# Moving the byte phase of the matmul streams and of the weights' low halves in a two-block hybrid network

## The chip, the cores and the metric

The kernel runs on one core of one Trainium2 chip. The metric is the device time of one execution in microseconds (us), taken as the median of several runs. TensorE does the matrix products, VectorE (DVE), ScalarE (ACT) and GpSimd (POOL) do elementwise work, and SyncE's queue (SP) issues the DMA transfers from device memory (HBM) into the on-chip buffer (SBUF, 128 partitions). TensorE writes its results into PSUM.

## The reference

The input is one sequence of 256 tokens with 2048 features in float32. Two residual blocks follow, and each is a mixer and a gated feed-forward network of width 5632, with an RMS norm ahead of each and one at the end:

```python
for i in range(DEPTH):                       # DEPTH = 2
    if i % 2 == 0:
        h = h + conv_pool_mixer(h, ...)      # w_in 2048x3072, 31-tap conv, pooling, w_out 2048x2048
    else:
        h = h + short_conv_mixer(h, ...)     # w_in 2048x6144, 3-tap conv, w_out 2048x2048
    h = h + swiglu(rms_norm(h, ffn_norm[i]), w_gate[i], w_up[i], w_down[i])
return rms_norm(h, final_norm)
```

All weights together are 5904 blocks of 128x128 float32, 387 MB, and each block is used for exactly one product with the 256 tokens.

## The kernel before

**Two halves for each number.** TensorE gets its operands in the type float32r, into which float32 is rounded. To keep the precision, each weight block and each activation is split: the high half is the rounded value, the low half is the float32 remainder, rounded in its turn. A product is hi times x-hi, plus hi times x-lo, plus lo times x-hi.

**How a product is issued.** `product` (lines 171 to 178) has two forms. The narrow one issues three matmuls of 256 columns (lines 176 to 178), each with its own weight load, all into one accumulator. It serves mixer 0 and the last output chunk of the last projection. The wide one issues two matmuls: the high weights against 512 columns (x-hi and x-lo side by side, line 173), and the low weights against the 256 columns of x-hi (line 174), which go into the second half of the accumulator. It serves everything else. TensorE loads the weights of a matmul while the matmul before it still streams: the low block is loaded while line 173 streams 512 columns, and the next product's high block while line 174 streams 256.

**How the weights come.** SP's queue fetches units of 16 blocks (1 MB) into four tiles `w` (line 114). `prepare` (lines 116 to 132) makes pieces of 8 blocks: ScalarE rounds `w` into a tile `hi` (line 124), and VectorE, or GpSimd for some pieces of mixer 0, subtracts into a tile `lo` (line 131). There are six tiles of each, and pieces are prepared four ahead. The blocks lie one behind another in a tile, 512 bytes each per partition. The order of the work is written out in the program: `next_block` hands out one block after another, and `tick` lets elementwise steps of mixer 0 in between.

**How the activations lie.** A stream is a chunk of 512 columns, 2048 bytes per partition: 1024 bytes of high halves and 1024 of low halves. Chunks lie one behind another in a room that is a little larger than they need; `moving(room, at, n)` (line 222) starts them `at` bytes into the room. The rooms are `xs` (the normed input of each mixer and network), `cat` (mixer 0's output), `y` (the hidden layer of a feed-forward network, one half of its width at a time) and `z` (the short-convolution mixer's output).

**Where everything lies.** Tiles are packed per partition one behind another, pool after pool, in steps of 32 bytes. All blocks and chunks have sizes that are multiples of 512, so one number per tile, its start modulo 512, says how a stream lies against the weights. Before the change the starts are, in bytes of a partition:

| what | start of the tile | offset `at` | modulo 512 | past the high halves, modulo 512 |
|---|---|---|---|---|
| hi (6 tiles of 4096) | 101952 | | 64 | 0 |
| lo (6 tiles of 4096) | 126528 | | 64 | 0 |
| w (4 tiles of 8192) | 69184 | | 64 | 0 |
| xs in mixer 0 (narrow) | 36160 | 32 | 352 | 288 |
| xs in the wide part | 36160 | 160 | 480 | 416 |
| cat (narrow) | 184928 | 0 | 96 | 32 |
| y (wide) | 159392 | 64 | 224 | 160 |
| z (wide) | 159392 | 64 | 224 | 160 |

The pools are laid down in the order constants, `h`, `xs`, `w`, `hi`, `lo`, small temporaries, and then what belongs to one phase (`cat`, `y` or `z` among it).

Of the kernel before, what the change touches and what calls it, by code (L numbers as in the profile page):

```python
# [12 lines left out]
F32R = mybir.dt.float32r  # L13
# [4 lines left out]
P = 128  # L18
T = 256
D = 2048  # L20
NC = D // P
# [4 lines left out]
NH = NF // 2  # L26
# [38 lines left out]
UNIT_AT = [sum(UNITS[:u]) for u in range(len(UNITS))]  # L65

PIECE = 8
PIECES = [(u, o, min(PIECE, n - o)) for u, n in enumerate(UNITS) for o in range(0, n, PIECE)]

LOOK = 4  # L70
AHEAD = 1

# [3 lines left out]


XS_M0 = 32
XS_F0 = 160
XS_M1 = 160  # L80
XS_F1 = 160
Y_F0 = 64
Y_F1 = 64
Z_M1 = 64
CAT = 0

POOL_SPLIT = range(96, 24 * NC + 16 + 7 * NC + 8)
# [7 lines left out]
def block_kernel(ctx: ExitStack, tc: tile.TileContext, xT: bass.AP, xtok: bass.AP, vec: bass.AP, wall: bass.AP, out: bass.AP):  # L95
    nc = tc.nc
    const = ctx.enter_context(tc.tile_pool(name="const", bufs=1))
    act = ctx.enter_context(tc.tile_pool(name="act", bufs=1))
    wst = ctx.enter_context(tc.tile_pool(name="wst", bufs=4))
    whl = ctx.enter_context(tc.tile_pool(name="whl", bufs=6))  # L100
# [9 lines left out]
    def fetch(u):  # L110
        if u < len(UNITS) and u not in loaded:
            n, off = UNITS[u], UNIT_AT[u] * P * P
            loaded[u] = w = wst.tile([P, 16 * P], F32, name="w")
            nc.sync.dma_start(w[:, : n * P], wall[off : off + n * P * P].rearrange("(p f) -> p f", p=P))  # L114

    def prepare(i):
        if i >= len(PIECES) or i in ready:
            return
        u, o, n = PIECES[i]
        fetch(u)  # L120
        w = loaded[u][:, o * P : (o + n) * P]
        hi = whl.tile([P, PIECE * P], F32R, name="hi")
        lo = whl.tile([P, PIECE * P], F32R, name="lo")
        nc.scalar.copy(hi[:, : n * P], w)  # L124
        engine = nc.vector
        if UNIT_AT[u] + o in POOL_SPLIT:
            if relief:
                relief.pop()
            else:
                engine = nc.gpsimd  # L130
        engine.tensor_tensor(out=lo[:, : n * P], in0=w, in1=hi[:, : n * P], op=ALU.subtract)  # L131
        ready[i] = (hi, lo)

    def next_block():
        b, i = cursor
        at = UNIT_AT[PIECES[i][0]] + PIECES[i][1]
        if b == at + PIECES[i][2]:
            ready.pop(i)
            i, at = i + 1, b
        for j in range(i, i + LOOK + 1):  # L140
            prepare(j)
        if i + LOOK < len(PIECES):
            for u in range(PIECES[i + LOOK][0] + 1, PIECES[i + LOOK][0] + AHEAD + 1):
                fetch(u)
        cursor[:] = [b + 1, i]
        hi, lo = ready[i]
        o = (b - at) * P
        return hi[:, o : o + P], lo[:, o : o + P]
# [16 lines left out]
    def drain():  # L165
        while any(queues.values()):
            for q in queues.values():
                if q:
                    q.popleft()[1]()
# [10 lines left out]
    def matmul_chunks(xs, ks, n=1, wide=False, behind=None):  # L180


        accs = [ps.tile([P, 2 * T], F32, name="acc") for _ in range(n)]
        for i, k in enumerate(ks):
            first, last = i == 0, i == len(ks) - 1
            for acc in accs:
                hi, lo = next_block()
                product(acc, hi, lo, xs[:, k, :], first, last, wide)
                tick()
            if behind is not None:  # L190
                behind(k)
        return accs
# [10 lines left out]
    def split(dst, src, scale=None):  # L203

        if scale is None:
            nc.scalar.copy(dst[:, :T], src)
            nc.vector.tensor_tensor(out=dst[:, T:], in0=src, in1=dst[:, :T], op=ALU.subtract)
        else:
            nc.scalar.activation(dst[:, :T], src, AF.Copy, scale=scale)
            nc.vector.scalar_tensor_tensor(out=dst[:, T:], in0=src, scalar=scale, in1=dst[:, :T], op0=ALU.mult, op1=ALU.subtract)  # L210
# [6 lines left out]

    identity = v[:, VECS["identity"] :]
    h = act.tile([P, NC, T], F32, name="h")
    xs_room = act.tile([P, NC * 2 * T + 64], F32R, name="xs")  # L220

    def moving(room, at, n):

        return room[:, at // 4 : at // 4 + n * 2 * T].rearrange("p (c t) -> p c t", c=n)
# [99 lines left out]
    def project(src, ks, norm=None, wide=False, narrow_end=False):  # L324

        for n in range(NC):
            if narrow_end and n == NC - 1:
                wide = False
            (acc,) = matmul_chunks(src, ks, wide=wide)
            if wide:  # L330
                t = phase[0].tile([P, T], F32, name="cross", bufs=3)
                nc.scalar.copy(t, acc[:, T:])
                nc.vector.tensor_tensor(out=h[:, n, :], in0=h[:, n, :], in1=t, op=ALU.add)
            nc.vector.tensor_tensor(out=h[:, n, :], in0=acc[:, :T], in1=h[:, n, :], op=ALU.add)  # L334
            if norm is not None:
                norm.add(n)

    def scaled(acc, r, name, wide=False):
        if not wide:
            s = (phase[0] if name == "pv" else tmp).tile([P, T], F32, name=name, bufs=2)  # L340
            nc.vector.tensor_tensor(out=s, in0=acc[:, :T], in1=r, op=ALU.mult)
            return s
        s = summed(acc, name)
        nc.vector.tensor_tensor(out=s, in0=s, in1=r, op=ALU.mult)
        return s
# [3 lines left out]
    xs = norm.xs  # L349
# [20 lines left out]
    rowsq = const.tile([P, 2], F32, name="rowsq")  # L370
    load(0, 1)
    prepare(0)
    prepare(1)
    load(1, 1)
    prepare(2)
# [8 lines left out]
    with tc.tile_pool(name="m0", bufs=1) as m0, tc.tile_pool(name="ps_side", bufs=2, space=PSUM) as ps_side:  # L384
# [166 lines left out]
        drain()  # L551
        norm = Norm("ffn_norm0", XS_F0)
        project(cat, range(NA), norm)

    def swiglu(norm, following, at):
        with tc.tile_pool(name="ffn", bufs=1) as fp:
            phase[0] = fp
            y = moving(fp.tile([P, NH * 2 * T + 32], F32R, name="y"), at, NH)
            r = None
            for half in range(2):  # L560
                for f in range(NH):
                    (acc_g,) = matmul_chunks(norm.xs, every, wide=True)
                    (acc_u,) = matmul_chunks(norm.xs, every, wide=True)
                    if r is None:
                        r = norm.rstd()
                    gate = scaled(acc_g, r, "gate", True)
                    up = scaled(acc_u, r, "val", True)
                    nc.scalar.activation(gate, gate, AF.Silu)
                    nc.vector.tensor_tensor(out=up, in0=up, in1=gate, op=ALU.mult)
                    split(y[:, f, :], up)  # L570
                project(y, range(NH), following if half else None, wide=True, narrow_end=half and following.final)
# [3 lines left out]

    after = Norm("mix_norm_o", XS_M1)
    swiglu(norm, after, Y_F0)


    norm = Norm("ffn_norm1", XS_F1)  # L580
    with tc.tile_pool(name="m1", bufs=1) as m1:
        phase[0] = m1
        z = moving(m1.tile([P, NC * 2 * T + 32], F32R, name="z"), Z_M1, NC)
        pad = SW - 1
        r = None
        for c in range(NC):
            (acc_c,) = matmul_chunks(after.xs, every, wide=True)
            (acc_v,) = matmul_chunks(after.xs, every, wide=True)
            if r is None:
                r = after.rstd()  # L590
            cg = scaled(acc_c, r, "gate", True)
            vv = scaled(acc_v, r, "val", True)
            cv = m1.tile([P, pad + T], F32, name="cv", bufs=2)
            nc.gpsimd.memset(cv[:, :pad], 0.0)
            nc.vector.tensor_tensor(out=cv[:, pad:], in0=cg, in1=vv, op=ALU.mult)
            wc = VECS["conv_w_o"] + c * SW
            co = m1.tile([P, T], F32, name="co", bufs=2)
            nc.vector.tensor_scalar(out=co, in0=cv[:, :T], scalar1=v[:, wc : wc + 1], scalar2=None, op0=ALU.mult)
            for k in range(1, SW):
                nc.vector.scalar_tensor_tensor(out=co, in0=cv[:, k : k + T], scalar=v[:, wc + k : wc + k + 1], in1=co, op0=ALU.mult, op1=ALU.add)  # L600
            (acc_b,) = matmul_chunks(after.xs, every, wide=True)
            bg = scaled(acc_b, r, "pv", True)
            nc.vector.tensor_tensor(out=bg, in0=bg, in1=co, op=ALU.mult)
            split(z[:, c, :], bg)
        project(z, every, norm, wide=True)


    last = Norm("final_norm", final=True)
    swiglu(norm, last, Y_F1)
    halves = rsqrt_of(*last.sums, scale=1.0 / D, halves=True)  # L610
    with tc.tile_pool(name="fin", bufs=1) as fin:
# [91 lines left out]
```

## Time and profile before

| | |
|---|---|
| median of 3 runs | 2094.08 us (2093.9 to 2096.47) |
| the profiled execution | 2094.95 us, of which the span from first to last instruction is 2093.2 us |
| TensorE matmul busy | 2070.2 us, 99% of the span, mean granted clock 0.996 |
| weight loads busy (overlapping the matmuls) | 1850.5 us, 88% |
| VectorE, ScalarE, GpSimd busy | 66%, 51%, 10% |
| read from HBM | 391.39 MB, 188 GB/s over the span |

A group of instructions is given as line, engine, operation, output and inputs, shape and count, then the busy time in us and the mean duration of one in ns, then the engine's idle time just before and what ended it. PE is TensorE's matmul side and PEld its weight loads. Matmuls are pipelined: one takes longer from start to end than the distance between the starts of two, so the distance is what sets the time. A row of the timeline has the start in us, the duration in us, the engine, the line and the instruction.

### The profile page before, as it was taken

The page shows a single profiled execution, that of the slowest core. Times are in us where ns is not written, and L with a number is a line of the kernel's source. Part 1 is how long each engine was busy: PE and PEld are TensorE (multiplying, and loading weights), DVE is VectorE, ACT ScalarE, POOL GpSimd, SP SyncE. Part 2 cuts the span into 40 slices and gives each one's busy share as a digit, 9 for nine tenths or more (in the row PEclk, how much of TensorE's full clock was granted, in tenths as well). Part 3 has the DMA queues.
Part 4 walks back from the last instruction along what each step waited for, and adds up shares of the span by engine and source line. Part 5 has one row for each costly group of instructions (what it writes and reads, how often), then busy time and mean ns, then how long its engine had stood idle before and what let it go on. Part 6 is the DMA issues. An engine that isn't in the chain of part 4 may idle for free.

```text
span 2093.2 us, 31608 instructions
## 1 busy us (share of the span) xinstructions
PE 2070.2 (99%) x12584; PEld 1850.5 (88%) x12584; DVE 1383.1 (66%) x1979; ACT 1061.8 (51%) x1571; POOL 200.5 (10%) x180
## 2 busy tenths in 40 slices
PE   8998999999999999999999999999999999999998
PEld 8998988888888888888888888888888888888887
DVE  6998766666556666666777777766666556666654
ACT  7886654444444444455444445554444444444453
POOL 2995200000000000011000001100000000000011
PEclk9999999999999999999999999999999999999999
DMA  8555455555555455555555555455555555555551
GB/s 322 190 199 181 151 190 184 193 189 186 196 184 198 182 195 188 188 195 183 189 191 184 198 182 199 181 186 197 182 195 187 190 193 184 199 183 195 187 191 71
DMA packets 56884, 395.53 MB, mean 189 GB/s; under 512 B 6432, under 2 KB 7200, under 8 KB 9760
## 3 DMA queue, kind: packets, MB, share of 16 engines
q1 hardware_dynamic: 56736, 393.52, 51.9%
q8 instruction: 98, 1.61, 0.3%
q14 instruction: 50, 0.41, 0.1%
HBM read 391.39 MB, written 2.10 MB: 188 GB/s over the span
## 4 chain that ended last, share of the span: by engine, by line
PE 98%; DMA 1%; DVE 1%; ACT 0%; SPq 0%; issue 0%; DVEq 0%; ACTq 0%
PE acc L173 57%; PE acc L174 29%; PE acc L176 4%; PE acc L178 4%; PE acc L177 3%; DMA rows<-in_xtok 0%; DMA h<-in_xT 0%; DVE res L620 0%; ACT hi L124 0%; PE st L252 0%; DVE lo L131 0%; PE st L283 0%; SPq L114 0%; ACT conv L492 0%; PE idle L258 0%
## 5 line engine op out<-in xcount | busy, mean ns | idle before, releaser
L131 DVE TENSOR_TENSOR lo<-w,hi 128x1024 fp32r<-128x1024 f32 (+1 forms) x691 | 846.2, 1225 | 634.3 <-ACT hi L124 630.1
L124 ACT CAST hi<-w 128x1024 fp32r<-128x1024 f32 (+1 forms) x740 | 775.5, 1049 | 963.9 <-PE acc L173 615.9
L173 PE MATMUL acc<-xs,hi 128*128 128x512 f32 x3584 | 1243.2, 392 | 0.0
L174 PE MATMUL acc<-xs,lo 128*128 128x256 f32 x3584 | 1002.3, 280 | 0.0
L173 PEld LDWEIGHTS acc<-xs,hi 128*128 128x128 f32 x3584 | 672.7, 188 | 148.5
L174 PEld LDWEIGHTS acc<-xs,lo 128*128 128x128 f32 x3584 | 672.7, 188 | 0.1
L173 PE MATMUL acc<-y,hi 128*128 128x512 f32 x1386 | 480.4, 392 | 0.0
L174 PE MATMUL acc<-y,lo 128*128 128x256 f32 x1386 | 386.8, 280 | 0.0
L173 PEld LDWEIGHTS acc<-y,hi 128*128 128x128 f32 x1386 | 259.9, 188 | 57.2
L174 PEld LDWEIGHTS acc<-y,lo 128*128 128x128 f32 x1386 | 260.2, 188 | 0.4
L314 POOL TENSOR_TENSOR sumsq<-sumsq,sq 128x256 f32<-128x256 f32 x56 | 59.0, 1053 | 1593.0 <-ACT sq L312 1593.0
L176 PE MATMUL acc<-xs,hi 128*128 128x256 f32 x512 | 142.7, 282 | 5.2 <-ACT hi L124 4.2
L177 PE MATMUL acc<-xs,hi 128*128 128x256 f32 x512 | 142.2, 280 | 0.0
L178 PE MATMUL acc<-xs,lo 128*128 128x256 f32 x512 | 140.2, 282 | 0.1
L131 POOL TENSOR_TENSOR lo<-w,hi 128x1024 fp32r<-128x1024 f32 x49 | 118.5, 2440 | 41.4 <-ACT hi L124 41.3
L176 PEld LDWEIGHTS acc<-xs,hi 128*128 128x128 f32 x512 | 96.9, 190 | 6.1 <-ACT hi L124 4.8
L177 PEld LDWEIGHTS acc<-xs,hi 128*128 128x128 f32 x512 | 96.9, 189 | 0.0
L178 PEld LDWEIGHTS acc<-xs,lo 128*128 128x128 f32 x512 | 95.4, 190 | 0.5 <-DVE lo L131 0.5
L173 PE MATMUL acc<-z,hi 128*128 128x512 f32 x256 | 88.7, 392 | 0.0
L198 ACT COPY cross<-acc 128x256 f32<-128x256 f32 x224 | 81.4, 363 | 0.0
L174 PE MATMUL acc<-z,lo 128*128 128x256 f32 x256 | 71.4, 280 | 0.0
L334 DVE TENSOR_TENSOR h<-acc,h 128x256 f32<-128x256 f32 x112 | 47.2, 423 | 18.3 <-PE acc L178 11.9
(134 smaller groups left out, 1199.3 us busy)
## 6 DMA issues: line engine op xcount, KB each, us to landing
w<-in_wall SPq DMA_DIRECT2D x365, 1024.0 KB, 4.8
w<-in_wall SPq DMA_DIRECT2D x7, 512.0 KB, 7.3
rows<-in_xtok SPq DMA_DIRECT2D x2, 1024.0 KB, 8.1
h<-in_xT SPq DMA_DIRECT2D x7, 256.0 KB, 7.2
out<-res SPq DMA_DIRECT2D x2, 512.0 KB, 2.8
out<-res SPq DMA_DIRECT2D x2, 384.0 KB, 2.8
v<-in_vec SPq DMA_DIRECT2D x1, 260.0 KB, 6.6
h<-in_xT SPq DMA_DIRECT2D x2, 128.0 KB, 2.3
```

The costliest lines, as they stand in the source:

```text
L124: nc.scalar.copy(hi[:, : n * P], w)
L131: engine.tensor_tensor(out=lo[:, : n * P], in0=w, in1=hi[:, : n * P], op=ALU.subtract)
L173: nc.tensor.matmul(acc, hi, x, start=first, stop=False, skip_group_check=True)
L174: nc.tensor.matmul(acc[:, T:], lo, x[:, :T], start=False, stop=last, skip_group_check=True)
L176: nc.tensor.matmul(acc[:, :T], hi, x[:, :T], start=first, stop=False)
L177: nc.tensor.matmul(acc[:, :T], hi, x[:, T:], start=False, stop=False)
L178: nc.tensor.matmul(acc[:, :T], lo, x[:, :T], start=False, stop=last)
L198: nc.scalar.copy(t, acc[:, T:])
L314: nc.gpsimd.tensor_tensor(out=self.sums[0], in0=self.sums[0], in1=sq, op=ALU.add)
L334: nc.vector.tensor_tensor(out=h[:, n, :], in0=acc[:, :T], in1=h[:, n, :], op=ALU.add)
```

## The change

Nothing is added to or taken from the list of instructions; addresses change.

- The room `xs` grows from 64 to 128 spare elements, 256 bytes, so all that is laid down after it moves up by 256.
- Each `lo` tile grows by 128 elements, 512 bytes. In the wide part (blocks from 656 on) its data begins 192 bytes into the tile; in mixer 0 it begins at its start as before.
- The rooms `y` and `z` grow from 32 to 128 spare elements.
- The offsets of `xs` in the wide part go from 160 to 416, those of `y` and `z` from 64 to 320. `XS_M0` stays 32 and `CAT` stays 0.
- `y` may have its own offset for each half; both are 320. `_ffn` is not used.

```diff
+_m0, _ffn = 24 * NC + 16 + NC * NC, 3 * NH * NC
+LO_AT = {0: 0, _m0: 192}
 XS_M0 = 32
-XS_F0 = 160
-XS_M1 = 160
-XS_F1 = 160
-Y_F0 = 64
-Y_F1 = 64
-Z_M1 = 64
+XS_F0 = 416
+XS_M1 = 416
+XS_F1 = 416
+Y_F0 = (320, 320)
+Y_F1 = (320, 320)
+Z_M1 = 320
...
-        lo = whl.tile([P, PIECE * P], F32R, name="lo")
+        lo = whl.tile([P, PIECE * P + 128], F32R, name="lo")
+        at = LO_AT[max(b for b in LO_AT if b <= UNIT_AT[u] + o)] // 4
+        lo = lo[:, at : at + PIECE * P]
...
-    xs_room = act.tile([P, NC * 2 * T + 64], F32R, name="xs")
+    xs_room = act.tile([P, NC * 2 * T + 128], F32R, name="xs")
...
-            y = moving(fp.tile([P, NH * 2 * T + 32], F32R, name="y"), at, NH)
+            y_room = fp.tile([P, NH * 2 * T + 128], F32R, name="y")
             r = None
             for half in range(2):
+                y = moving(y_room, at[half], NH)
...
-        z = moving(m1.tile([P, NC * 2 * T + 32], F32R, name="z"), Z_M1, NC)
+        z = moving(m1.tile([P, NC * 2 * T + 128], F32R, name="z"), Z_M1, NC)
```

## The prediction

> **What bounds the kernel now.** I read the page's first and fourth parts first, then the groups by line and shape, then the timeline of TensorE in stretches without a gap.
>
> ```profile
> span 2093.2 us, 31608 instructions
> PE 2070.2 (99%) x12584; PEld 1850.5 (88%) x12584; DVE 1383.1 (66%) x1979; ACT 1061.8 (51%) x1571; POOL 200.5 (10%) x180
> PE 98%; DMA 1%; DVE 1%; ACT 0%; SPq 0%; issue 0%; DVEq 0%; ACTq 0%
> ```
>
> The chain that ends last is TensorE for 98% of the span. What does not change the pace of the matmuls, or stop them, does not change the time. The groups say which matmuls these are:
>
> ```profile
> L173 PE MATMUL acc<-xs,hi 128*128 128x512 f32 x3584 | 1243.2, 392 | 0.0
> L174 PE MATMUL acc<-xs,lo 128*128 128x256 f32 x3584 | 1002.3, 280 | 0.0
> L173 PE MATMUL acc<-y,hi 128*128 128x512 f32 x1386 | 480.4, 392 | 0.0
> L173 PE MATMUL acc<-z,hi 128*128 128x512 f32 x256 | 88.7, 392 | 0.0
> L131 DVE TENSOR_TENSOR lo<-w,hi 128x1024 fp32r<-128x1024 f32 x688 | 844.6, 1228 | 632.3 <-ACT hi L124 628.1 <-PE acc L174 3.6
> L174 PEld LDWEIGHTS acc<-xs,lo 128*128 128x128 f32 x3584 | 672.7, 188 | 0.1
> ```
>
> There are 3584 + 1386 + 256 = 5226 wide products, and no wide matmul waited for anything (idle 0.0). Their pace is read from starts. First a stretch of the timeline on `xs`, with its first two and last two rows; between them lie 59 pairs:
>
> ```profile
> 299.80 0.39 PE L173 MATMUL acc<-xs,hi 128*128 128x512 f32 x1
> 300.03 0.28 PE L174 MATMUL acc<-xs,lo 128*128 128x256 f32 x1
> ...
> 320.26 0.39 PE L173 MATMUL acc<-xs,hi 128*128 128x512 f32 x1
> 320.49 0.28 PE L174 MATMUL acc<-xs,lo 128*128 128x256 f32 x1
> ```
>
> 59 pairs in 20.46 us are 346.8 ns a pair. Over these 59 the mean distance from a line 173 to its line 174 is 229.2 ns (so much for 512 columns), and the rest, 117.6 ns, is the slot of the 256 columns. Then the same on `y`, first and last row, 44 pairs apart:
>
> ```profile
> 519.61 0.39 PE L173 MATMUL acc<-y,hi 128*128 128x512 f32 x1
> ...
> 534.86 0.39 PE L173 MATMUL acc<-y,hi 128*128 128x512 f32 x1
> ```
>
> That is 15.25 us / 44 = 346.6 ns. 5226 pairs at 346.7 ns make 1812 us of the 2093.2. One nanosecond a pair is 5.2 us, 0.25% of the time.
>
> **Is there time in a pair that is not the streaming itself?** A row of matmuls of another kind answers, the sums over features and the fillers at the end, which are plain float32:
>
> ```profile
> L283 PE MATMUL st<-diag,ones x10: 378/379/454, 40.3 to 1365.8; 128*128 128x256 f32 x10
> L258 PE MATMUL idle<-ones x16: 275/275/356, 2081.6 to 2083.4; 128*128 128x128 f32 x16
> 275.84 0.43 PE st L283 x2
> ```
>
> In the program there are five matmuls of line 283, and ten records: a float32 product runs as two records, and the third line (the chain of waits) gives 0.43 us for two, 0.215 each, nearly twice the 112 ns by which 392 exceeds 280. So such a record occupies the array about as a 512-column matmul would, and it lasts 379 where line 173 lasts 392; by the same reading line 258 lasts 275 where line 174 lasts 280. The wide matmuls thus carry some 13 and 5 ns that a stream of the same length need not have. What they are the trace does not say. A weight load runs beside each of them from its start, as the timeline has it for one pair:
>
> ```profile
> 742.17 0.39 PE L173 MATMUL acc<-xs,hi 128*128 128x512 f32 x1
> 742.17 0.19 PEld L174 LDWEIGHTS acc<-xs,lo 128*128 128x128 f32 x1
> 742.40 0.28 PE L174 MATMUL acc<-xs,lo 128*128 128x256 f32 x1
> 742.40 0.19 PEld L173 LDWEIGHTS acc<-xs,hi 128*128 128x128 f32 x1
> ```
>
> The stream and the load read two places of one memory at the same time, and their getting in each other's way is the candidate.
>
> **The change part by part.**
>
> *Phase of the streams on `xs`.* The room `xs` keeps its start; `hi` moves up by 256 (the room's growth), the offset by 416 - 160 = 256. Past the high halves it stays at 416. Cost nothing: nothing moves against anything.
>
> *Phase of `y` and `z`.* Their base moves up by 256 (the room `xs`) and 6 x 512 (the `lo` tiles), which is 256 modulo 512, as `hi` does; the offset goes from 64 to 320. So they go from 160 to 416. The trace has both phases: 346.8 ns at 416 (`xs`) and 346.6 at 160 (`y`). 1642 pairs times 0.2 ns is 0.3 us: nothing.
>
> *Phase of `xs` in mixer 0.* The offset stays, `hi` moves: 288 becomes 32, which is where `cat` is now. Both are in the trace, first the narrow products on `xs`, 93 starts apart, then those on `cat`, 96 apart:
>
> ```profile
> 127.84 0.28 PE L176 MATMUL acc<-xs,hi 128*128 128x256 f32 x1
> ...
> 138.68 0.28 PE L176 MATMUL acc<-xs,hi 128*128 128x256 f32 x1
> ```
>
> ```profile
> 241.80 0.28 PE L176 MATMUL acc<-cat,hi 128*128 128x256 f32 x1
> ...
> 253.00 0.28 PE L176 MATMUL acc<-cat,hi 128*128 128x256 f32 x1
> ```
>
> 10.84 / 93 = 116.6 ns and 11.20 / 96 = 116.7 ns. Cost nothing.
>
> *The low halves, 192 bytes on.* This is the one new thing. Until now `lo` and `hi` had the same phase everywhere, so no row shows a stream against two different ones. What changes is which bytes the load of a low block reads while line 173 streams: the stream lies 416 - 192 = 224 past the low halves instead of 416 (or 160). Under line 174 the next high block is loaded, at 416 as before. So the slot of 117.6 ns stays, and the slot of 229.2 is in play. Its bounds: on the good side line 173 falls to what line 283 shows, 392 - 379 = 13 ns x 5226 = 67.9 us saved. On the bad side the load costs the stream as much again, 13 ns more, 67.9 us lost. For a value between I take the stream's own marginal pace: 392 - 280 = 112 ns per 256 columns, so 512 columns take 224, and 229.2 - 224 = 5.2 ns is what the slot holds beyond it. I take these 5.2 ns as saved, because the slot of line 173 is the only one in which a stall can sit in front of a second half that no load disturbs: the load of 128 columns starts with the matmul, and the last columns of 512 stream alone. 5.2 x 5226 = 27.2 us.
>
> The Trainium skill speaks against this. "SBUF — State Buffer" (section "Who interferes with whom") gives TensorE two independent read ports, one for the moving operand and one for weight loads, and says that PE never waits on anyone; by it the phase is worth nothing and the sum is 0. Its page "TensorE: Matmul & The Clock Gate" (section "Wait — 56ns, not 53.3ns?") gives a warm matmul N / 2.4 GHz + about 2.5 ns, an estimate of 325 ns for a pair; the trace has 346.7 at a granted clock of 1.00, so here something costs 22 ns a pair that neither rule names.
>
> *Elementwise work.* VectorE writes `lo` at another phase; `w` and `hi`, which it reads, keep theirs to each other. ScalarE's work is the same. Price zero, and the cover is this window of the first feed-forward network and the mixer behind it (columns: PE, PEld, DVE, ACT, POOL busy, clock, DMA share, GB/s):
>
> ```profile
> 330.00:1150.00 820.00, 820.00 (x4735) 721.92 (x4734) 530.29 (x722) 388.10 (x551) 15.08 (x25) 1.00 0.52 189
> ```
>
> VectorE is idle for 290 of 820 us; a piece of 8 blocks takes TensorE 8 x 346.7 = 2774 ns, so there are 296 pieces and 0.98 us of slack for each. The subtraction of 1228 ns would have to become some 2.2 us before TensorE waited. A faster TensorE takes slack away: at 341.5 ns a pair 42 ns per piece. The DMA share would go from 0.52 to 0.53. No buffer is taken away and no wait added: every tile keeps its number of buffers.
>
> *Sum.* The profiled execution took 2094.95 us (2093.2 of it span); less 27.2 that is 2067.8. The median of the runs, 2094.08, lies 0.9 below it, so I predict 2067 us.
>
> **The rivals.**
>
> *Nothing moves (2094 us).* Each pair of phases in the trace gives one pace: 416 and 160 wide, 288 and 32 narrow. If no phase at all matters and the 13 ns belong to the float32r stream itself, the shift of `lo` is one more number without effect. For it: those four, and that the pace is the same in all wide stages. Against it: the two members of each pair differ by exactly 256, so a pattern that repeats every 256 bytes would hide in them, and 192 is no multiple of that. The Trainium skill's rule of separate ports is this rival. It takes in the case that the change does not do what it says (that the phases come out as before), which I think excluded by the starts.
>
> *Slower: the low load meets the stream.* Place: line 173, the load of the low block beside it. At the new distance of 224 the load and the stream go to the same part of the memory more often than at 416, and each meeting holds up the stream. It decides as soon as the new distance stalls the stream longer than the old one. Price by the rows: another 5.2 ns a pair gives 2094 + 27 = 2121 us, 13 ns gives 2162. If the stall were small, 1 ns, 2099. For it: the distance has never been in this trace. Against it: the old distance has no sign of being a best one either, with 13 ns over line 283.
>
> *The whole of it goes (2026 us).* Line 173 falls to 379 ns: 2094 - 68. For it: a stall that has one cause goes as a whole. Against it: line 174 keeps its 5 ns at the unchanged distance, so some of the excess belongs to any load beside a stream.
>
> **How the numbers follow.** Part of the stall goes (the forecast, 2067, and by itself from 2035 to 2089): 0.48. All of it goes: 0.08. Nothing moves: 0.27. Slower: 0.17. What this kernel's measurement tells from no change is about 0.2%, 4 us, so faster has 0.48 + 0.08 = 0.56, the same 0.27, slower 0.17. The range goes down to the bound 2026 and up past no change to 2106, which holds the slower case with up to 2.3 ns a pair; what lies beyond is 0.13 above and about 0.03 below.
>
> **What would show it.** In the changed trace the distance from line 173 to line 174 is the test: 224 ns instead of 229.2, with line 174 to the next line 173 still at 117 to 118, and the same for `xs`, `y` and `z`. The duration of line 173 should fall under 392. The narrow stage up to 256 us should end when it did, within 1 us. Line 131 on VectorE may move by some ns and nobody waits for it. I am wrong if the slot of line 174 is what changes (then the load of the high block was the one in the way), if `xs` and `y` come apart, or if TensorE shows new idle time ahead of line 173 or 174.

## The result and the profile after

The changed kernel takes 2103.49 us (median of 5 runs, 2103.14 to 2106.32) against 2096.47 us for the kernel before (median of its 5 runs, 2093.90 to 2096.86). The ratio is 1.0042, with a 95% interval of 1.0031 to 1.0053. It is slower by some 7 to 9 us: the medians differ by 7.0 and the spans of the two profiled executions by 8.2 (2101.4 us against 2093.2), and the ratio stands for 8.8. One execution of the fourteen kernels is left out of all ratios: of the four of the kernel described below that has streams and low halves at 64, one took 10228 us and the others 2059 to 2062, and no trace shows why.

The new code lines move the products: the line 173 of before is line 178, line 174 is 179, and line 131 is 136. First the head of the page of the changed kernel and its groups of the wide matmuls and of the subtraction:

```profile
span 2101.4 us, 31608 instructions
PE 2079.6 (99%) x12584; PEld 1852.1 (88%) x12584; DVE 1383.8 (66%) x1979; ACT 1061.3 (51%) x1571; POOL 200.5 (10%) x180
...
L178 PE MATMUL acc<-xs,hi 128*128 128x512 f32 x3584 | 1249.3, 393 | 0.0
L179 PE MATMUL acc<-xs,lo 128*128 128x256 f32 x3584 | 1002.7, 280 | 0.0
L178 PE MATMUL acc<-y,hi 128*128 128x512 f32 x1386 | 481.7, 393 | 0.0
L178 PE MATMUL acc<-z,hi 128*128 128x512 f32 x256 | 90.1, 396 | 0.0
L136 DVE TENSOR_TENSOR lo<-w,hi 128x1024 fp32r<-128x1024 f32 x688 | 844.9, 1229 | 638.7 <-ACT hi L129 634.4 <-PE acc L179 3.7
```

The work is the same, the counts are the same, and still no wide matmul waits (idle 0.0). What was lost lies in the pace, the distance from the start of one pair to the start of the next: line 178 lasts 393 to 396 ns where it lasted 392. But a mean hides what happened. These are TensorE's matmuls in five stretches of 100 us, first before (columns: stretch in us, its length, busy time and number of matmuls, granted clock, DMA share, GB/s):

```profile
300.00:400.00 100.00, 100.00 (x579) 1.00 0.52 190
600.00:700.00 100.00, 100.00 (x579) 1.00 0.53 190
1100.00:1200.00 100.00, 100.00 (x579) 1.00 0.53 190
1400.00:1500.00 100.00, 100.00 (x579) 1.00 0.53 190
1700.00:1800.00 100.00, 100.00 (x579) 1.00 0.52 190
```

and the same stretches after:

```profile
300.00:400.00 100.00, 100.00 (x570) 1.00 0.53 189
600.00:700.00 100.00, 100.00 (x585) 1.00 0.53 190
1100.00:1200.00 100.00, 100.00 (x570) 1.00 0.52 184
1400.00:1500.00 100.00, 100.00 (x570) 1.00 0.52 184
1700.00:1800.00 100.00, 100.00 (x584) 1.00 0.54 194
```

Before, every stretch holds 579 (2 x 100 / 0.3467 = 577, and those that reach over the edges). After, some hold fewer (570) and some more (584 or 585), at the same granted clock of 1.00, on the same tile `xs` and at the same phases. The timeline of the changed kernel gives both paces; a pace that holds for a whole stretch is called a cadence from here on. First row and last row of line 178 in a stretch of the slow kind, 50 pairs apart, and in one of the fast kind, 51 pairs apart:

```profile
299.87 0.40 PE L178 MATMUL acc<-xs,hi 128*128 128x512 f32 x1
...
317.47 0.40 PE L178 MATMUL acc<-xs,hi 128*128 128x512 f32 x1
...
699.66 0.39 PE L178 MATMUL acc<-xs,hi 128*128 128x512 f32 x1
...
717.17 0.39 PE L178 MATMUL acc<-xs,hi 128*128 128x512 f32 x1
```

17.60 / 50 = 352.0 ns and 17.51 / 51 = 343.3 ns a pair; before it was 346.7 everywhere. The mean distance from line 178 to line 179 is 234.2 ns at the slow cadence and 226.7 at the fast cadence (229.2 before), so most of the difference lies in the slot of the 512 columns.

Taken over the whole trace, the slow cadence holds from the spread of the first norm (275.6 us) to 513.8, from 876.3 to 1610.8 and from 1973.3 to the end of the wide part. Inside the second of these stretches the 19 pairs between the sums and the spread of a norm are fast, twice (from 1003.7 and from 1365.3 us). Everywhere else the fast cadence holds. Of 5206 pairs whose neighbours are regular, 3010 have the slow cadence and 2196 the fast one. 3010 x (352.0 - 346.7) = 16.0 us lost and 2196 x (346.7 - 343.35) = 7.3 us won (343.35 is the mean of the 2196) leave 8.7 us. The narrow part ended 0.45 us earlier (the first wide matmul starts at 256.05 instead of 256.50). That makes 8.25 us; the span grew by 8.2.

Where does the cadence change? Around 513.8 us the regular order high, low, high, low is broken. This is the changed kernel's timeline there:

```profile
513.18 0.40 PE L178 MATMUL acc<-y,hi 128*128 128x512 f32 x1
513.42 0.28 PE L179 MATMUL acc<-y,lo 128*128 128x256 f32 x1
513.54 0.63 PE L178 MATMUL acc<-y,hi 128*128 128x512 f32 x2
514.01 0.40 PE L179 MATMUL acc<-y,lo 128*128 128x256 f32 x2
514.25 0.40 PE L178 MATMUL acc<-y,hi 128*128 128x512 f32 x1
```

Two long matmuls follow each other and then two short ones. Probably the last product of the first output chunk, which needs the last chunk of `y`, is put between the halves of a product of the second; the trace does not name the chunks. Both kernels have five such places, one behind the start of each projection on `y` and `z`. At the head of three stages the order is broken twice more, by the sums of the norm (line 257) and, 20 pairs on, by their spread (line 288), which brings the norm's factors to all partitions. All changes of cadence lie at these eleven places. Not every place changes it: the sums of the first norm and the place on `z` did not.

### The profile page after: what moved, and what is told of

Read it like the earlier page. It is cut to its first block, busy times and chain, and to the rows that moved or that the text cites. A ratio compares the mean times of both kernels' runs of the same rounds, so it can differ in the third digit from the quotient of the medians.

```text
span 2101.4 us, 31608 instructions
## 1 busy us (share of the span) xinstructions
PE 2079.6 (99%) x12584; PEld 1852.1 (88%) x12584; DVE 1383.8 (66%) x1979; ACT 1061.3 (51%) x1571; POOL 200.5 (10%) x180
## 4 chain that ended last, share of the span: by engine, by line
PE 98%; DMA 1%; DVE 1%; ACT 0%; SPq 0%; issue 0%; DVEq 0%; ACTq 0%
PE acc L178 57%; PE acc L179 29%; PE acc L181 4%; PE acc L183 4%; PE acc L182 3%; DMA rows<-in_xtok 0%; DMA h<-in_xT 0%; DVE res L626 0%; ACT hi L129 0%; PE st L257 0%; DVE lo L136 0%; PE st L288 0%; SPq L117 0%; ACT conv L497 0%; PE idle L263 0%
```

## Experiments

Theory A: the shift of the low halves splits the pace into two cadences, and which one holds is a state that only an irregular place can change. Its rivals: B, the moved streams have a part in it; C, the two distances (stream past high halves, stream past low halves) set one pace each; D, the stage or the other engines' work in it decides; E, VectorE's writes at the new phase are in the way.

### The change in two halves

The first kernel undoes the shift of the low halves alone:

```diff
-LO_AT = {0: 0, _m0: 192}
+LO_AT = {0: 0, _m0: 0}
```

> The changed kernel with the low halves put back to the high ones' phase (offset 0 in the wide part too); the layout and the phases of the streams stay as changed (416 everywhere in the wide part, 32 in mixer 0). Theory A, the shift of the low halves alone splits the pace of the wide pairs into two cadences (343.3 and 352.0 ns in the changed trace): this kernel has one cadence again, 346.7 ns in xs, y and z, and takes the time of before within 0.2% (2090 to 2099 us). Rival B, the move of y and z from 160 to 416 or of mixer 0 from 288 to 32 has a part in it: two cadences or a pace other than 346.7 ns remain on y or z, or the narrow stage ends elsewhere, and the time stays 4 us or more above before.

Measured: 2094.62 us against 2094.34 before, ratio 1.0001 (0.9991 to 1.0011), one cadence at 346.7 ns in all wide stages.

The second puts that shift alone into the kernel before; streams stay at 416 on `xs` and 160 on `y` and `z`:

```diff
-        lo = whl.tile([P, PIECE * P], F32R, name="lo")
+        lo = whl.tile([P, PIECE * P + 128], F32R, name="lo")
+        at = LO_AT[max(b for b in LO_AT if b <= UNIT_AT[u] + o)] // 4
+        lo = lo[:, at : at + PIECE * P]
```

> The kernel before with nothing but the low halves of the wide part 192 bytes on: xs at 416 past the high halves (224 past the low ones), y and z at 160 past the high halves (480 past the low ones). Theory A: the stages on xs run at 343.3 or 352.0 ns a pair as in the changed kernel. If only the phase modulo 256 counts, y and z do so too and the time is that of the changed kernel, 2100 to 2106 us; if 512 counts, y and z have a pace of their own, and the stages on xs still show the two cadences. Rival B: without the moved y and z the pace on xs is 346.7 ns and the time that of before.

Measured: 2104.16 us, ratio 1.0047 (1.0032 to 1.0062). The trace has the same two cadences in the same stages, on `y` at 160 as on `y` at 416; only the first 31 pairs differ, which ran at 352 here and at 343.6 in the changed kernel. The whole loss belongs to the low halves, and B falls. For these cells only the phase modulo 256 counts.

### All distances in one run

Two kernels sweep the phases inside one execution. The streams' phases differ by stage, and `lo` begins at a place that depends on the block:

```diff
-LO_AT = {0: 0, _m0: 192}
+def low_at(b):
+    ...
+    start, n = max(s for s in STEPS if s[0] <= b)
+    i = (b - start) // n
+    return 32 * i if i < 16 else 192
...
-        at = LO_AT[max(b for b in LO_AT if b <= UNIT_AT[u] + o)] // 4
+        at = low_at(UNIT_AT[u] + o) // 4
```

> The changed kernel with the phases swept inside one run: in each wide stage the low halves go from 0 to 480 bytes past the high ones in steps of 32 (16 to 48 products each), and the stages' streams lie at 416, 0, 64, 128, 192, 256, 320 and 384 past the high halves (first network: xs 416, y 0 and 64; mixer 1: xs 128, z 192; second network: xs 256, y 320 and 384). Theory C, the two distances (stream to high, stream to low) set the pace: line by line the pair takes different times, between 341 and 360 ns, and the same pair of distances gives the same pace wherever it stands. Theory A, there are two cadences at one and the same pair of distances and the way in decides: some neighbours in the sweep keep a cadence over a change of the distance. If the two reads don't meet at all: 346.7 ns everywhere.

> The same sweep with the streams at the odd multiples of 32: first network xs 160, y 32 and 96; mixer 1 xs 224, z 288; second network xs 352, y 416 and 480. Theory C: the map goes on smoothly between the columns of the other sweep; the column 160 is like 416 where the low halves are not shifted (346.7 ns, as y before), and differs where 512 counts. Theory A: at 416 on y and a shift of 192 either 343.3 or 352.0 ns, not a value between. If the two reads don't meet at all: 346.7 ns everywhere.

Measured: 2108.46 and 2111.58 us (one run each). The table has the ns of a pair, the mean over the second half of each stretch, worked out from the starts in the two traces. Stretches that hold an irregular place are left out. Rows are the stream past the high halves, columns the low halves past the high ones, both modulo 256. Values that lie more than 1.2 ns apart in one cell are set side by side.

| | 0 | 32 | 64 | 96 | 128 | 160 | 192 | 224 |
|---|---|---|---|---|---|---|---|---|
| 0 | 347 / 354 | 347 | 347 | 347 | 347 | 347 | 351 | 353 |
| 32 | 347 | 347 | 349 | 347 | 347 | 350 | 347 / 353 | 353 |
| 64 | 349 / 354 | 349 | 340 / 350 | 347 | 347 | 349 | 347 | 350 |
| 96 | 350 | 353 | 347 | 349 | 347 | 349 | 353 | 347 |
| 128 | 351 | 351 | 347 | 347 | 352 | 351 | 347 | 352 |
| 160 | 347 | 351 | 353 | 348 | 353 | 347 | 352 | 347 / 348 |
| 192 | 353 | 353 | 350 | 347 / 353 | 353 | 350 | 340 | 347 |
| 224 | 347 / 353 | 348 / 351 | 347 / 350 / 353 | 347 / 353 | 350 | 351 | 347 / 350 | 352 |

The kernel before stands in row 160, column 0; the changed one in row 160, column 192. Of 312 stretches 122 lie within 0.5 ns of 346.7, 183 above 348 and 4 below 346, all four at 340.0. So phases do matter, a shift taken blindly is more likely to lose than to win, and the same cell can have two paces. C holds for most cells and fails for some: (64, 64) ran at 340.0 and at 350.0. There the low halves lay at 64 and at 320, but the next sweep has 350.0 at 64 too, so a phase modulo 512 is not the reason. In both sweeps the changed kernel's cell showed only its slow cadence, in every visit.

A third sweep goes in steps of 8 bytes around the two cells at 340.0; its edit is the same with other numbers (shown against the first sweep):

```diff
-    return 32 * i if i < 16 else 192
+    return ((128, 120, 128, 136, 144, 112, 0, 8, 0, 504)[STEPS.index((start, n))] + 8 * min(i, 15)) % 512
```

> A sweep like the two before, in steps of 8 bytes around the cells that ran at 340.0: streams at 192, 184, 200, 208 and 176 past the high halves in the first network and mixer 1, 64, 72 and 56 in the second network; the low halves go from 64 below the stream to 56 above it (the stream 64 to -56 past the low halves). Theory C: around 0 there is a stretch of some 16 to 48 bytes at 340 ns and no pair below it, and outside it up to 353. If 340 is not a floor, some cell goes below, down to 325 ns.

Measured: 2113.92 us (one run). There is no stretch of fast cells. With the stream at 192, the low halves 40 below the stream, 16 below it and 40 above it give 340.0, and the cells between give 347 to 353. Among these is (192, 192) itself, which had 340.0 in the first sweep and has 353 here, both times it comes up. Streams at 184, 200, 72 and 56, which are no multiples of 16, never reach 340; they lie between 346.6 and 366.6. But those at 208, 176 and 64, which are multiples of 16, do not reach it here either (346.5 to 355.5). Nothing goes below 340.0. The width that C expected is refuted, its floor held.

### Two cells applied everywhere

Both kernels change numbers only; this is the first, whose low halves stay 192 bytes on. The second has 64 in place of each 192, for the low halves too, and 480 in place of 96, which places `y` and `z` at 64.

```diff
-XS_F0 = 416
-XS_M1 = 416
-XS_F1 = 416
+XS_F0 = 192
+XS_M1 = 192
+XS_F1 = 192
...
-Y_F0 = (320, 320)
-Y_F1 = (320, 320)
-Z_M1 = 320
+Y_F0 = (96, 96)
+Y_F1 = (96, 96)
+Z_M1 = 96
```

> The changed kernel with other phases: all wide streams at 192 past the high halves (instead of 416), low halves 192 on as there, so that the stream lies at 0 past the low halves. In the sweep this cell ran at 340.0 ns a pair in mixer 1's z, both times it came up. Theory C (the two distances set the pace, with one cadence here): 340.0 ns in every wide stage, 5226 x 6.67 = 34.9 us under before, 2058 to 2062 us. Theory A (two cadences here too): 340 ns in some stages and 345 to 353 in others, 2065 to 2110 us.

Measured: 2111.81 us, ratio 1.0087 (1.0073 to 1.0101). Ahead of the first norm's sums 28 pairs ran at 340.0, and from these sums on all ran at 350.0. The cell that had 340.0 twice in the first sweep makes the slowest of the kernels with one set of phases.

> The changed kernel with all wide streams at 64 past the high halves and the low halves 64 on; again the stream lies at 0 past the low halves. In the sweep the cell (64, 64) and its like (320, 64) ran at 340.0 ns, the cells (64, 320) and (320, 320), which are the same modulo 256, at 350.0. Theory A: two cadences, 340.0 and 350.0, which change at the irregular places only, and a time between 2060 and 2112 us. Theory C: if 512 counts for the low halves, 340.0 throughout, 2058 to 2062 us.

Measured: 2061.57 us against 2094.67, ratio 0.9839 (0.9824 to 0.9854). This beats both kernels. Its groups and its timeline, 51 pairs between first and last row:

```profile
L178 PE MATMUL acc<-xs,hi 128*128 128x512 f32 x3584 | 1220.3, 389 | 0.0
L179 PE MATMUL acc<-xs,lo 128*128 128x256 f32 x3584 | 990.2, 276 | 0.0
```

```profile
699.83 0.39 PE L178 MATMUL acc<-xs,hi 128*128 128x512 f32 x1
...
717.17 0.39 PE L178 MATMUL acc<-xs,hi 128*128 128x512 f32 x1
```

17.34 / 51 = 340.0 ns, in every wide stage, but not for all of it. The first 31 wide pairs ran at 350.0, and so did the 19 pairs between the sums and the spread of each of the three norms. These are the first and the last of the 19 behind the second norm's sums, 18 pairs apart:

```profile
988.74 0.40 PE L178 MATMUL acc<-xs,hi 128*128 128x512 f32 x1
...
995.04 0.40 PE L178 MATMUL acc<-xs,hi 128*128 128x512 f32 x1
```

6.30 / 18 = 350.0 ns. So this kernel has two cadences at one and the same phases as well: the sums of the second and third norm led from 340.0 into 350.0, and the spread led back each time. At (192, 192) the spread did not lead back. Both kinds of matmul are shorter than before (389 for 392, 276 for 280).

### Does an irregular place switch the cadence?

The changed kernel gets more irregular places, with the phases untouched. In every third accumulator on `xs` and `z` one low matmul is issued after the next product:

```diff
-                product(acc, hi, lo, xs[:, k, :], first, last, wide)
+                x = xs[:, k, :]
+                if nests and i == 5:
+                    nc.tensor.matmul(acc, hi, x, start=False, stop=False, skip_group_check=True)
+                    held = lo, x
+                    tick()
+                    continue
+                product(acc, hi, lo, x, first, last, wide)
+                if nests and i == 6:
+                    nc.tensor.matmul(acc[:, T:], held[0], held[1][:, :T], start=False, stop=False, skip_group_check=True)
```

> The changed kernel, its phases as they are, with 40 more irregular places: in every third accumulator of the stages on xs the sixth product's low matmul is issued after the seventh product's two (high, high, low, low instead of high, low, high, low). Same work, same operands. Theory A, the cadence is a state that holds until the regular order of long and short streams is broken: between two such places the pace is either 343.3 or 352.0 ns and nothing else, it changes at such places and nowhere else, and the fast one turns up in stages that had only the slow one (first network before 513 us, mixer 1). Rival D, the stage or what the other engines do in it decides: 352.0 from 276 to 513 us and from 876 to 1610, 343.3 from 513 to 876 and from 1611 to 1973, as in the changed kernel, nests or not.

The places are 80 and not 40 as the expectation has it (75 on `xs`, 5 on `z`). Measured: 2100.61 us (one run). This is the timeline around one of them, with the held matmul in line 197 and its low half in line 203:

```profile
353.20 0.39 PE L178 MATMUL acc<-xs,hi 128*128 128x512 f32 x1
353.43 0.28 PE L179 MATMUL acc<-xs,lo 128*128 128x256 f32 x1
353.54 0.39 PE L178 MATMUL acc<-xs,hi 128*128 128x512 f32 x1
353.77 0.28 PE L179 MATMUL acc<-xs,lo 128*128 128x256 f32 x1
353.89 0.39 PE L197 MATMUL acc<-xs,hi 128*128 128x512 f32 x1
354.12 0.39 PE L178 MATMUL acc<-xs,hi 128*128 128x512 f32 x1
354.35 0.28 PE L179 MATMUL acc<-xs,lo 128*128 128x256 f32 x1
354.46 0.28 PE L203 MATMUL acc<-xs,lo 128*128 128x256 f32 x1
354.58 0.40 PE L178 MATMUL acc<-xs,hi 128*128 128x512 f32 x1
354.81 0.28 PE L179 MATMUL acc<-xs,lo 128*128 128x256 f32 x1
354.93 0.40 PE L178 MATMUL acc<-xs,hi 128*128 128x512 f32 x1
355.17 0.28 PE L179 MATMUL acc<-xs,lo 128*128 128x256 f32 x1
355.28 0.40 PE L178 MATMUL acc<-xs,hi 128*128 128x512 f32 x1
```

Ahead of the place the pairs take 0.34 us and line 178 lasts 0.39; behind it they take 0.35 and it lasts 0.40, at once and until the next place. Where places lie 48 pairs apart in a row, the cadence alternates between 343.3 and 352.0 in every stage, in those that had only one cadence in the changed kernel too. A few places did not switch: the second one of the first network, one on `z`, and the kernel's own one at the first projection of the second network. D falls.

### Holding the fast cadence on purpose

If the state is the cause, a few places at the right points must turn the changed kernel into a faster one, with its phases as they are. The first try has eight:

```diff
+NESTS = (53, 704 + 73, 1760 + 73, 2112 + 53, 2880 + 73, 3136 + 53, 3840 + 73, 4896 + 73)
...
+                if wide and count[0] in NESTS:
+                    nc.tensor.matmul(acc, hi, x, start=False, stop=False, skip_group_check=True)
+                    held = lo, x
...
```

> The changed kernel, its phases as they are, with eight more irregular places, chosen from the run with forty: one close behind the sums of each norm (the 54th wide pair of the stage) and one 48 pairs behind each of the five places where the changed kernel has one of its own. Theory A: the slow cadence then lasts for some 20 pairs behind each of three norms and 48 behind each of the five places, about 300 of 5226; the others run at 343.3 ns. 4920 x 3.33 = 16.4 us won and 300 x 5.33 = 1.6 lost against 346.7: 2078 to 2084 us, faster than before. Where a place fails to switch, its stretch stays at 352.0 and each 100 pairs cost 0.9 us more. Rival D (the stage decides) or a cause in the phases alone: 2102 to 2106 us as in the changed kernel.

Measured: 2099.22 us, ratio 1.0021 (1.0012 to 1.0031), slower than before and not faster. The trace says which places failed. The three behind the norms came right after the spread and left the cadence at 352.0, so the stages on `xs` stayed slow but for the second half of each network. The five that lie 48 pairs behind a place of the kernel's own all switched; the one on `z` switched the wrong way, because the kernel's own place had already made it fast. 2570 pairs are slow and 2620 fast, which is 2570 x 5.3 - 2620 x 3.35 = 4.8 us over 346.7; the wide part began 0.85 us earlier, and the span is 4.1 over that of before. Up to the first of the new places this program is that of the changed kernel, instruction by instruction, and yet its first 31 pairs ran at 352 and not at 343.6: what the cadence is at the entry differs from one execution to another.

The second try replaces the places behind the norms by those that had worked among the 80, with what lay ahead of them:

```diff
-NESTS = (53, 704 + 73, 1760 + 73, 2112 + 53, 2880 + 73, 3136 + 53, 3840 + 73, 4896 + 73)
+NESTS = (
+    37, 85, 133, 704 + 73, 1760 + 73, 2112 + 21, 2112 + 69, 2880 + 73, 3136 + 5, 3136 + 53, 3840 + 73, 4896 + 73,
+)
```

> The changed kernel, its phases as they are, with twelve more irregular places: behind the norms those that were followed by the fast cadence in the run with forty (pairs 37, 85 and 133 of the first network, 21 and 69 of mixer 1, 5 and 53 of the second network, counted in their stage), and one 48 pairs behind each of the five places of the changed kernel, as in the run with eight. Theory A, with the state carried on from place to place: the slow cadence lasts for some 100 + 30 + 20 pairs behind the norms and 48 behind each of the five, about 400 of 5226. 4800 x 3.33 = 16.0 us won, 400 x 5.33 = 2.1 lost: 2079 to 2085 us, faster than before. If a place fails to switch, its stage stays at 352.0: first network up to its first place 3.8 us, mixer 1 and second network as much each. Rival D: 2099 to 2106 us.

Measured: 2081.17 us against 2094.62, ratio 0.9944 (0.9927 to 0.9961), inside the expected 2079 to 2085. Two of its ten executions took 2091.21 and 2094.19 us, though; the other eight lie between 2079.74 and 2081.36. The two have no trace, so it is not shown what happened in them; 10 and 13 us would be an estimated 1150 and 1500 pairs at 352.0 instead of 343.35. This is TensorE in the profiled execution, one of the eight, in the stretches shown above:

```profile
300.00:400.00 100.00, 100.00 (x583) 1.00 0.52 191
600.00:700.00 100.00, 100.00 (x585) 1.00 0.54 195
...
1100.00:1200.00 100.00, 100.00 (x584) 1.00 0.52 191
1400.00:1500.00 100.00, 100.00 (x585) 1.00 0.54 194
1700.00:1800.00 100.00, 100.00 (x584) 1.00 0.53 190
```

All are of the fast kind now (the first still has slow pairs up to 305 us); 4790 pairs are fast and 392 slow (400 were expected). With the phases of the changed kernel and the same matmuls, the order of a few of them decides between 0.4% slower and 0.6% faster in most executions.

Does the kernel at (64, 64) owe its 340.0 to luck in this? It gets the 80 places as well, by the edit shown above for them.

> The kernel with streams at 64 and low halves at 64, which ran at 340.0 ns throughout, with the forty irregular places of the other run (every third accumulator on xs and z). Theory A: this cell has a second cadence too, 350.0 ns by the sweeps, and the places reach it: stretches at 340.0 and at 350.0, nothing between, and a time between 2061 and 2095 us. If 340.0 is the only cadence of this cell, it holds everywhere and the time is 2059 to 2064 us; then the 350.0 in the sweeps came from their other low halves.

Measured: 2062.76 us (one run), which lies in both expected ranges. Behind almost every one of the 80 places three pairs take longer (some 351, 347 and 345 ns) and then 340.0 holds again. 350.0 turns up where it did without the new places: in the first 31 pairs and between the sums and the spread of each norm. So this cell has a second cadence, as theory A says, and 340.0 is not its only one; but these places lead neither into it nor, at the one place that fell into it (the 38th pair), out of it. The kernel owes its time to the spread of the norms, which led back to 340.0 each time, and nothing here tells that beforehand.

### TensorE's reads or VectorE's writes?

```diff
-            nc.tensor.matmul(acc[:, T:], lo, x[:, :T], start=False, stop=last, skip_group_check=True)
+            nc.tensor.matmul(acc[:, T:], hi, x[:, :T], start=False, stop=last, skip_group_check=True)
```

> The changed kernel, but in the wide products the second matmul is fed from the high block instead of the low one; the low halves are still computed and written 192 bytes on, and nothing reads them. The product of the low weights is left out and that of the high weights counted twice, so the output is not the reference's. What TensorE reads now has one phase, as before the change; what VectorE writes has the changed one. Theory A/C, TensorE's own weight load beside its stream: one cadence, 346.7 ns a pair, as before. Rival E, VectorE's writes at their new phase get in TensorE's way: the two cadences 343.3 and 352.0 ns as in the changed kernel. If the loads with one and the same block in a row were left out by the chip, the number of weight loads in the trace falls from 12584 and the pace is below 346.7.

Measured: 2095.61 us (one run), 2094.62 before. The head of its page, and line 178 on the timeline, 51 pairs from first to last:

```profile
PE 2070.3 (99%) x12584; PEld 1850.9 (88%) x12584; DVE 1385.8 (66%) x1979; ACT 1062.2 (51%) x1571; POOL 196.8 (9%) x180
```

```profile
699.72 0.39 PE L178 MATMUL acc<-xs,hi 128*128 128x512 f32 x1
...
717.40 0.39 PE L178 MATMUL acc<-xs,hi 128*128 128x512 f32 x1
```

17.68 / 51 = 346.7 ns, in one cadence, with all 12584 weight loads there. The five places on `y` and `z` are regular in this kernel, so it says nothing on the switching; but neither 343.3 nor 352.0 turns up, not even behind the norms. The writes 192 bytes on are harmless; it is where TensorE reads its weights that makes the two cadences. E falls.

## Why the prediction was wrong

**What bounds the kernel.** Right: a wide pair's pace was the only thing that moved, no wide matmul waits in either trace, and the pairs' sum accounts for the span to 0.1 us.

**The streams' phases at no cost.** Right for all three steps: with the low halves put back, the ratio is 1.0001.

**Elementwise work at no cost.** Right: VectorE is busy for 1383.8 us against 1383.1, no wide matmul waits for it, and its writes alone change nothing.

**The low halves: the step that failed.** I took 5.2 ns as saved, because "the slot of line 173 is the only one in which a stall can sit in front of a second half that no load disturbs". This has two faults. The first is the sign: nothing in the trace said that the new distance is better than the old one. The reason I gave tells where a stall can sit, not which distance makes it smaller. The sweeps show that 346.7 is one of the better paces (183 of 312 stretches lie above 348, 4 below 346). The second is that I took one pace for one distance. The slot of 229.2 became 226.7 at one cadence and 234.2 at the other, 2.5 ns saved and 5.0 ns lost; only the mixture, 3010 pairs at the slow cadence to 2196 at the fast, made the result 0.42% slower. The size was no better founded: the 224 ns of bare streaming is twice the difference of two durations, whose ends the profile models, and the shortest mean slot of a whole kernel is some 227; nor did line 178 come near the bound of 379, with 389 as its shortest mean.

**Which slot.** Right in the main: the slot of line 174 went from 117.5 ns to 116.7 in the fast cadence and 117.8 in the slow one. It is not fixed, though: in the kernel at (64, 64), where the stream also lies elsewhere past the high halves, it is some 113 ns.

**The rivals.** "Nothing moves" rested on paces that agree at distances 256 apart; the period is indeed 256 where both were run, as the argument against it said. "Slower: the low load meets the stream" had the right place and, with 5.2 ns a pair, nearly the price of the slow cadence (5.3); it would have come to some 2122 us if that cadence had held everywhere. That the measured time lies inside the range up to 2106 is luck: the two cadences nearly balanced. None of the cases had a pace that depends on the past. The 0.17 for slower was too little.

**The rule of the Trainium skill.** "SBUF — State Buffer" (section "Who interferes with whom") has TensorE wait on nobody. The runs differ: in whole kernels the same matmuls take 340.0 to 352.0 ns a pair, by the places of their operands and by the order of a few of them. In the kernel that moves the low halves alone, the weight loads are the only reads of TensorE that moved. The same page's table of specifications (section "Specifications (TRN2)") speaks of cachelines of 16 bytes; that streams off a multiple of 16 never reached 340 would fit it, but three of the four streams at multiples of 16 in the same sweep did not reach it either, so no run here shows that this is the reason. By "TensorE: Matmul & The Clock Gate" (section "Wait — 56ns, not 53.3ns?") a pair would take an estimated 325 ns; nothing here went below 340.0.

**What stays open.** What the state consists of was not found. That it changes only where the alternation of long and short streams is broken is shown, and that the places of operands decide which cadences there are. Which place switches and which does not was read from runs and never derived, and the try with eight places went wrong in just that. It is not fixed by the program alone either: the first 31 pairs, with the same program up to there, ran at some 344 in two profiled executions and at 352 in two others, and two of the ten executions with twelve places took 10 and 13 us longer. The step from 340.0 down to the bare streaming was not explained.

## What to carry to other kernels

Where weight loads run beside the streams and the matmuls bound the time, the places of the operands modulo 256 bytes are a parameter worth a per cent or two (here 0.984 to 1.009), and it can be swept inside a single run by giving each stretch of blocks its own offset. Read the pace from the starts of matmuls stretch by stretch, never as one mean, and judge a candidate in the whole kernel: the cell that looked best in a short stretch, 340.0 twice, ran at 350.0 when it was used throughout. Look at every execution and not at the median alone, since the cadence can differ between executions of one program. When two paces appear at the same phases, look for what breaks the regular order of the matmuls.

## What the hardware showed that was not expected

TensorE's cadence has a memory: at the same phases a pair took 343.3 or 352.0 ns for hundreds of pairs on end, and the exchange of one short matmul with the long one behind it switched it. The cadences are repeating patterns: at 352.0 five pairs of 358, 344, 352, 353 and 353 ns follow each other again and again, at 343.3 pairs of 345 and some 342 take turns, and at 340.0 all pairs are alike. With streams and low halves both at 64 (the stream at 0 past the low ones) the pace was 340.0 ns in all stages but for 88 pairs at 350.0, some 227 for the 512 columns and 113 for the 256; no run went below that.
